# The value weights of the scan: one place, asked for in two halves

## The chip, the cores and the metric

The kernel runs on one core of a Trainium2 chip. The metric is the device time of one execution in microseconds (us). Smaller is better.

## The reference, cut to what matters

The model is an encoder trunk with two layers. Each is a SwiGLU feed-forward, a token mixer and a second feed-forward, with layer norms between. The first layer's mixer is neighbourhood attention. The second's is a bidirectional RWKV-7 time mixing, and the change is in that one.

```python
def rwkv7_bidir(x, mix, w_rkv, ...):          # x: 1 x 512 tokens x 1024 channels
    ...
    xr, xw, xk, xv, xa, xg = (x + xx * mix[i] for i in range(6))
    r = xr @ w_rkv[0]
    k = xk @ w_rkv[1]
    v = xv @ w_rkv[2]                          # the value product
    ...
    def step(state, inp):                      # per direction, 16 heads of 64 channels
        r_t, w_t, k_t, v_t, a_t, b_t = inp
        sa = jnp.einsum('zbhij,zbhj->zbhi', state, a_t)
        state = state * w_t[..., None, :] + sa[..., None] * b_t[..., None, :] + v_t[..., None] * k_t[..., None, :]
        return state, jnp.einsum('zbhij,zbhj->zbhi', state, r_t)
    _, ys = lax.scan(step, jnp.zeros((2, B, H, N, N), f32), xs)
    ...
    return ((y + bonus) * g).astype(x.dtype) @ w_out
```

All numbers are float32.

## The kernel before

The trunk runs as one program of 2200 us: feed-forward, attention, two feed-forwards, the projections of the time mixing, the scan, its output product, and a last feed-forward. The scan takes the stretch from about 1418 to 1803 us.

**Pairs and slots.** The scan works on pairs of heads. A pair (`hp`, 0 to 7) is 128 channels, so it fills the 128 partitions. Tokens come in 8 chunks of 64. The method `slot(n)` runs once per pair, with n from -2 to 7, and in each slot several pairs are at different stages. In slot n the chunk chain runs for pair n (`chain`, thread `c`), the output of pair n - 1 is finished (`finish`, `gate`), the small triangular matrices of pair n + 1 are inverted to the end (`inverted`, `merge`), and for pair n + 2 the decays and factors are made (`front`), the grams, the start of the inversion (`invert`, on GpSimd) and the values (`values`, thread `v`). Pair n + 3 is loaded.

**The order.** Each thread is a generator that yields between its steps. A string per slot (`SEQ`) names the threads in the order in which their next step is written. For TensorE (PE), VectorE (DVE) and ScalarE (ACT) the program keeps that order by hand. GpSimd's (POOL) and SyncE's (SP) instructions are ordered by a planner, from its own estimate of times. SP issues all DMAs, one after the other, so an ask that waits holds back the asks behind it.

**The value product.** For one pair, `values` makes 128 channels x 512 tokens in a PSUM bank: 8 steps, one for each 128 input channels, each of four matmul rows in the trace (`wide`, L1255: two halves of the output channels). Its moving operand is the token tile `xv` (in the trace: `xraw`), its stationary operand the weight tile `wv`, 128 partitions x 8 x 128 numbers, 512 KB. The steps are spread over the slot, between those of the chain. The first `v` in a slot's string writes nothing. The next eight are the steps.

**The weight tile.** There is room for one (`bufs=1`). Behind the last step of a product `weigh` takes the place anew for the next pair and asks for all 512 KB (L1625). A tile that is taken anew waits for every reader of the former one, so the ask waits for the eighth step. The first pair's weights are asked for ahead of the scan's slots, in `receptances`. When the products are done, `outs` takes the place once more, for a part of the output weights (`w_out`).

**Other names that stand in the trace.** L1506 loads the decays `lw` for `front`. L1515 loads the receptance, L1485 and L1488 other inputs of a pair. L1591 and L1592 copy parts of the factors `ar` into the tiles `az` and `xs` that the chain reads. L1703 copies the inverted matrices to `az` in eight small DMAs; they are read by L1758 in the next slot. L1747 to L1766 are the chain: for each chunk, three matmul groups on PE (L1747, L1758, L1764) with ACT (L1751, L1759) between, and DVE's L1766, which makes the next state. L1686 and L1688 are the inversion on POOL, L1679 and L1698 the DVE transposes ahead of it and behind it. L1798 loads output chunks into the token tile `xv` in the slot of the last pair's values.

Of the kernel before, what the change touches and what calls it, by code (L numbers as in the profile page):

```python
# [18 lines left out]
P = 128  # L19
# [4 lines left out]
ND = D // P  # L24
# [78 lines left out]
def flat(ap):  # L103
    return ap.rearrange("p a b -> p (a b)")
# [1015 lines left out]
class Heads:  # L1120
# [114 lines left out]
    def values(self, hp, oT):  # L1235

        k, nc = self.k, self.nc
        po = k.bank()
        for b in range(NB):
            for c in range(2):  # L1240
                for hh in range(2):
                    hs = slice((2 * hp + hh) * HD, (2 * hp + hh + 1) * HD)
                    nc.tensor.matmul(po[HALF[hh], b * P : (b + 1) * P], self.v[b][c][:, hs],
                                     self.pt[hh, b // 2][:, b % 2, c * P : (c + 1) * P], start=c == 0, stop=c == 1)
            if b == NB - 1:
                k.split(*oT.get(hp), halves_of(po))
            yield


class Scan:  # L1250
# [78 lines left out]
    def receptances(self):  # L1329

        nc = self.nc
        one = lambda ap: ap.rearrange("p a b c d -> p (a b c d)")
        az = self.az[2].rearrange("p a b c -> p (a b c)")
        xr = [h[:, i * S : (i + 1) * S] for h, n in ((az, 4), (one(self.units[-2][0]), 2), (one(self.units[-1][0]), 2)) for i in range(n)]
        w = {}

        def load(hp, ap):
            w[hp] = ap.rearrange("p (c f) -> p c f", c=ND)
            self.asked = nc.sync.dma_start(ap, self.w_r[hp]).ins

        def chunk(c):
            nc.sync.dma_start(xr[c], self.dram["xr"][:, c, :])

        for n in ("mask", "onesb"):
            nc.sync.dma_start(getattr(self, n), self.consts[n])
        chunk(0)
        for hp, i in zip(WR_FIRST, (4, 5, 6, 7)):
            load(hp, one(self.units[i][0]))
            if hp == WR_FIRST[0]:
                for c in range(1, ND):  # L1350
                    chunk(c)
                yield
                with self.k.behind(self.asked):
                    self.weigh(0)
            elif hp == WR_FIRST[1]:
                yield
        for _ in range(2):
            self.unit()
        rest = [hp for hp in range(1, ND) if hp not in WR_FIRST]
        order = WR_FIRST + tuple(rest)  # L1360
        while rest:
            pair, rest = rest[:2], rest[2:]
            vt = self.tile("vt", [P, NC, 2, 2, CH], 2)
            for i, hp in enumerate(pair):
                load(hp, one(vt)[:, i * D : (i + 1) * D])
        for i, hp in enumerate(order):
            pr = self.k.bank("ym"[i % 2])
            for c in range(ND):
                self.wide(pr, w[hp][:, c, :], xr[c], c == 0, c == ND - 1)
                if c % 2 and c < ND - 1:  # L1370
                    yield
            t = self.tile(("yh", "yt")[hp % 2], [P, S])
            nc.scalar.activation(t, pr, AF.Copy)
            nc.sync.dma_start(self.dram["rkv"][0][:, hp, :], t)
            if hp == order[-1]:
                self.clear(2)
            yield
# [228 lines left out]
    def values(self, hp):  # L1606

        k, nc, tile_ = self.k, self.nc, self.tile
        p = self.st[hp]
        wv = self.wv  # L1610
        yield
        p.v = tile_("v", [P, S], 2)
        pv = k.bank("a")
        for c in range(ND):
            self.wide(pv, wv[:, c, :], self.xv[:, c, :], c == 0, c == ND - 1)
            if c < ND - 1:
                yield
        nc.scalar.activation(p.v, pv, AF.Copy)
        self.weigh(hp + 1)
        yield  # L1620

    def weigh(self, hp):
        if self.has(hp):
            self.wv = self.tile("wv", [P, ND, P])
            self.nc.sync.dma_start(flat(self.wv), self.w_v[hp])  # L1625

    def gates(self):

# [159 lines left out]
    def outs(self):  # L1788

        nc = self.nc  # L1790
        rows = lambda ap, k: ap[k * P : (k + 1) * P, :]
        w = [self.tile(n, [P, NC, 2, CH]).rearrange("p a b c -> p (a b c)") for n in ("bk1", "ar1")]
        w += [self.az[2][:, i].rearrange("p a b -> p (a b)") for i in range(2)]
        w += [self.tile("wv", [P, ND, P]).rearrange("p a b -> p (a b)")]
        w += [self.units[i][0].rearrange("p a b c d -> p (a b c d)") for i in (2, 4, 3)]
        self.w, self.left = w, [rows(self.dram["x"], t) for t in range(NT)]
        for i in range(EARLY - 1):
            nc.sync.dma_start(self.xv[:, i, :], self.dram["o"][:, i, :])  # L1798
            ask = nc.sync.dma_start(w[i], rows(self.w_out, i)).ins
        yield  # L1800
        for n, (t, h) in enumerate((t, h) for t in range(NT) for h in range(2)):
            hs = slice(h * 512, (h + 1) * 512)
            x = self.tile(("e", "e2", "th")[n % 3], [P, S], 2)
            nc.sync.dma_start(x, rows(self.dram["x"], t)[:, hs])
            acc = self.k.bank("ag"[n % 2])
            for i in range(EARLY):
                if n == 0 and i == EARLY - 1:
                    with self.k.behind(ask):
                        nc.sync.dma_start(self.xv[:, i, :], self.dram["o"][:, i, :])
                        nc.sync.dma_start(w[i], rows(self.w_out, i))  # L1810
                self.wide(acc, self.xv[:, i, t * P : (t + 1) * P], w[i][:, hs], i == 0, i == EARLY - 1)
                if i < EARLY - 1:
                    yield
            nc.vector.scalar_tensor_tensor(x, x, ALPHA, acc, ALU.mult, ALU.add)
            ask = nc.sync.dma_start(rows(self.dram["x"], t)[:, hs], x).ins
            if n == 0:
                with self.k.behind(ask):
                    for c in range(EARLY, ND - 1):
                        nc.sync.dma_start(w[c], rows(self.w_out, c))
            self.stored += 1  # L1820
            self.reload()
            yield
# [214 lines left out]
```

## Time and profile before

| | |
|---|---|
| three runs | 2205.87, 2207.17, 2219.66 us |
| median | 2207.17 us |
| profiled execution, its time | 2204.32 us |
| profiled execution, span from first to last instruction | 2201.7 us |
| mean granted TensorE clock | 0.991 |
| busy share of the span: PE, DVE, ACT, POOL | 97%, 70%, 49%, 24% |

The page's busy share is an average over all stages. A wait names the instruction that waited, and what ended last before it went on. A row of the timeline gives start and length in us, then engine, line, operation, tiles, shapes and count, and in brackets the idle time before it with the one that ended it. The granted clock is the share of full TensorE speed, which falls to 0.5 in some places.

### The profile page before, as it was taken

How to read it: one execution, taken by the hardware profiler on the slowest of the kernel's cores; microseconds unless marked ns; L12 is line 12 of the kernel's file. 1: busy time of each engine (PE TensorE's matmuls, PEld its weight loads, DVE VectorE, ACT ScalarE, POOL GpSimd, SP SyncE). 2: the span in 40 equal slices, each digit the busy share in tenths (PEclk: the TensorE clock that was granted, in tenths of full speed). 3: DMA queues.
4: the chain of work that ended last, by engine and by line, in shares of the span. 5: the costliest groups of instructions: out<-in, count | busy, mean ns of one | idle time of the engine just before them, and what ended most of it. 6: DMA issues, size and time to landing. Idle time of an engine off the chain costs nothing.

```text
span 2201.7 us, 38797 instructions
## 1 busy us (share of the span) xinstructions
PE 2131.1 (97%) x15248; PEld 1726.2 (78%) x15248; DVE 1551.5 (70%) x2506; ACT 1082.2 (49%) x1987; POOL 527.5 (24%) x670
## 2 busy tenths in 40 slices
PE   9999999999999999999999999999998999999998
PEld 8888888887888888787888877446666567788876
DVE  7777767377487777697777779636887558777775
ACT  4444445377344444453444444437776434444443
POOL 1000035555300000520000242046877610000023
PEclk9999999999999999999999999999999999999999
DMA  6544593432334556734555853853544551455583
GB/s 191 174 163 155 177 361 114 117 101 77 113 125 158 159 171 199 298 128 145 159 169 164 311 207 118 293 160 106 135 118 118 169 188 64 152 159 171 163 296 135
DMA packets 160805, 367.81 MB, mean 167 GB/s; under 512 B 32144, under 2 KB 52240, under 8 KB 158576
## 3 DMA queue, kind: packets, MB, share of 16 engines
q1 hardware_dynamic: 160624, 365.36, 50.9%
q8 instruction: 119, 1.95, 0.4%
q14 instruction: 62, 0.51, 0.1%
HBM read 284.29 MB, written 68.94 MB: 160 GB/s over the span
## 4 chain that ended last, share of the span: by engine, by line
PE 63%; DVE 18%; DMA 12%; ACT 3%; issue 2%; POOL 0%; SPq 0%; DVEq 0%; ACTq 0%; POOLq 0%
PE bank L980 13%; PE bank L1063 12%; DMA ra<-in_ffn_w_out_dram 7%; PE a L1255 5%; PE bank L288 5%; PE bank L287 5%; PE bank L289 5%; DVE w L278 4%; PE bank L350 4%; DVE ring L278 2%; ACT w L277 2%; DMA raw<-in_ffn_w_in_dram 2%; PE g L1579 1%; PE y L1255 1%; DVE wx L278 1%
## 5 line engine op out<-in xcount | busy, mean ns | idle before, releaser
L278 POOL TENSOR_TENSOR w<-raw,w 128x1024 fp32r<-128x1024 f32 x38 | 93.4, 2462 | 1206.5 <-ACT w L277 1200.2
L287 PE MATMUL bank<-xT,w 128*128 128x512 f32 x760 | 298.1, 392 | 6.5 <-DVE ar L497 6.5
L278 DVE TENSOR_TENSOR w<-raw,w 128x1024 fp32r<-128x1024 f32 x164 | 200.5, 1223 | 136.4 <-ACT w L277 134.6
L288 PE MATMUL bank<-xT,w 128*128 128x512 f32 x760 | 296.1, 390 | 0.0
L289 PE MATMUL bank<-xT,w 128*128 128x512 f32 x760 | 295.7, 389 | 0.0
L277 ACT ACTIVATE w<-raw 128x1024 fp32r<-128x1024 f32 x202 | 213.0, 1058 | 129.8 <-DMA raw<-in_ffn_w_in_dram 33.6
L1063 PE MATMUL bank<-wx,an 128*128 128x512 f32 x792 | 201.8, 392 | 0.0
L1063 PE MATMUL bank<-w,ring 128*128 128x512 f32 x720 | 171.8, 395 | 7.3 <-DVE w L278 7.3
L287 PEld LDWEIGHTS bank<-xT,w 128*128 128x128 f32 x760 | 142.7, 188 | 37.4 <-DVE ar L497 8.8
L277 ACT ACTIVATE ring<-raw 128x512 fp32r<-128x512 f32 (+1 forms) x99 | 89.3, 904 | 161.5 <-DVE raw L957 119.0
L1063 PEld LDWEIGHTS bank<-w,ring 128*128 128x128 f32 x720 | 136.7, 190 | 38.2 <-DVE w L278 9.0
L289 PEld LDWEIGHTS bank<-xT,w 128*128 128x128 f32 x760 | 142.7, 188 | 30.0
L288 PEld LDWEIGHTS bank<-xT,w 128*128 128x128 f32 x760 | 142.8, 188 | 28.4
L1063 PEld LDWEIGHTS bank<-wx,an 128*128 128x128 f32 x792 | 142.0, 189 | 24.7
L980 PEld LDWEIGHTS bank<-ring,w 128*128 128x128 f32 x864 | 110.8, 191 | 33.4 <-ACT bank L972 30.4
L980 PE MATMUL bank<-ring,w 128*128 128x256 f32 x864 | 119.0, 287 | 15.7 <-ACT bank L972 15.4
L1686 POOL TENSOR_TENSOR tm<-qs,zs 128x126 f32<-128x126 f32 (+22 forms) x248 | 102.8, 414 | 86.9 <-issue 38.9
L1688 POOL TENSOR_TENSOR zs<-zs,tm 128x126 f32<-128x126 f32 (+22 forms) x248 | 112.6, 454 | 19.4
L980 PE MATMUL bank<-ring 128*128 128x256 f32 x864 | 116.3, 284 | 0.1
L980 PEld LDWEIGHTS bank<-ring 128*128 128x128 f32 x864 | 109.6, 193 | 0.4 <-ACT tmp L972 0.4
L495 ACT ACTIVATE tmp<-bank 128x512 f32<-128x512 f32 x52 | 31.1, 597 | 151.8 <-PE bank L289 151.8
L980 PE MATMUL bank<-xT,w 128*128 128x256 f32 x756 | 100.6, 283 | 0.0
(383 smaller groups left out, 4679.4 us busy)
## 6 DMA issues: line engine op xcount, KB each, us to landing
raw<-in_ffn_w_in_dram SPq DMA_DIRECT2D x176, 512.0 KB, 3.7
ra<-in_ffn_w_out_dram SPq DMA_DIRECT2D x44, 1024.0 KB, 5.2
d_away<-away SPq DMA_DIRECT2D x44, 512.0 KB, 4.4
ring<-d_away SPq DMA_DIRECT2D x16, 1024.0 KB, 11.5
xT<-d_late SPq DMA_DIRECT2D x29, 512.0 KB, 8.3
xT<-in_ffn_w_out_dram SPq DMA_DIRECT2D x23, 512.0 KB, 10.0
d_late<-ts SPq DMA_DIRECT2D x44, 256.0 KB, 2.0
d_late<-ra SPq DMA_DIRECT2D x44, 256.0 KB, 2.0
```

Source lines behind the costliest of these rows:

```text
L277: self.hi = self.nc.scalar.activation(h, raw, AF.Copy).ins
L278: self.lo = (eng or self.nc.vector).tensor_tensor(l, raw, h.bitcast(F32), ALU.subtract).ins
L287: nc.tensor.matmul(out, wh, xh, start=start, stop=False)
L288: nc.tensor.matmul(out, wh, xl, start=False, stop=False)
L289: nc.tensor.matmul(out, wl, xh, start=False, stop=stop)
L350: nc.tensor.matmul(acc[t, h], a, u[:, i, h * 512 : (h + 1) * 512], start=first and n == 0, stop=last and n == 2)
L495: nc.scalar.activation(s, pg, AF.Silu)
L980: m = nc.tensor.matmul(out, w[:, i, cs], x[:, j, c], start=start and c + n == 0, stop=c == 3 and n == 2, skip_group_check=True)
L1063: self.nc.tensor.matmul(acc, lhs, u[:, i], start=bool(first) and m == 0, stop=last and m == 2, skip_group_check=more)
L1255: self.nc.tensor.matmul(out[hs], w[:, hs], x, start=start, stop=stop)
L1686: nc.gpsimd.tensor_tensor(tv, qs[:, s, 0:s].rearrange("p (a o) -> p a o", o=1).broadcast_to([P, s, n]), zs[:, s : s + 1, c0:].broadcast_to ...
L1688: nc.gpsimd.tensor_tensor(zs[:, 0:s, c0:], zs[:, 0:s, c0:], tv, ALU.add)
```

## The change

The weight tile is taken once, ahead of the scan, and kept in `self.wv`. The load of a pair's weights becomes two DMAs of 256 KB: input channels of steps 1 to 4, and of steps 5 to 8. The first is written behind the fourth step of the former pair's product, the second where the whole load was, behind the eighth. `outs` uses the kept tile instead of taking the place anew.

```diff
                 with self.k.behind(self.asked):
-                    self.weigh(0)
+                    self.wv = self.tile("wv", [P, ND, P])
+                    for half in range(2):
+                        self.weigh(0, half)
...
         for c in range(ND):
             self.wide(pv, wv[:, c, :], self.xv[:, c, :], c == 0, c == ND - 1)
+            if c == ND // 2 - 1:
+                self.weigh(hp + 1, 0)
             if c < ND - 1:
                 yield
         nc.scalar.activation(p.v, pv, AF.Copy)
-        self.weigh(hp + 1)
-        yield
-
-    def weigh(self, hp):
+        self.weigh(hp + 1, 1)
+        yield
+
+    def weigh(self, hp, half):
         if self.has(hp):
-            self.wv = self.tile("wv", [P, ND, P])
-            self.nc.sync.dma_start(flat(self.wv), self.w_v[hp])
+            cs = slice(half * ND // 2, (half + 1) * ND // 2)
+            self.nc.sync.dma_start(flat(self.wv[:, cs]), self.w_v[hp][:, cs.start * P : cs.stop * P])
...
-        w += [self.tile("wv", [P, ND, P]).rearrange("p a b -> p (a b)")]
+        w += [flat(self.wv)]
```

## The prediction

> **What bounds the kernel now.** I read the page first, then the waits of TensorE in the scan (1418 to 1803 us), then TensorE's rows around each wait. The first fence has the page's span and engines, then a windows row that covers one slot of the scan, the stretch in which pair 4 gets its values.
>
> ```profile
> span 2201.7 us, 38797 instructions
> PE 2131.1 (97%) x15248; PEld 1726.2 (78%) x15248; DVE 1551.5 (70%) x2506; ACT 1082.2 (49%) x1987; POOL 527.5 (24%) x670
> ```
>
> ```profile
> 1576.00:1612.00 36.00, 34.70 (x632) 25.20 (x631) 31.35 (x64) 28.52 (x78) 28.36 (x63) 1.00 0.48 129
> ```
>
> The columns after the length are busy time of PE, its weight loads, DVE, ACT and POOL, then the granted clock, the DMA share and GB/s. In these 36.00 us PE is busy 34.70. So 1.30 us is idle, and next to nothing else is. The other engines have 4.6 us or more left, and the DMA engines half their time. The slot is bound by PE's own list plus that one hole. Who makes the hole is in the waits of PE over the whole scan (us in total, times, longest):
>
> ```profile
> PE a L1255 <- DMA wv<-in_w_rv_dram: 8.9, 4, 3.4
> PE a L1255 <- DVE yt L1837: 2.4, 1, 2.4
> ```
>
> and in PE's timeline, where the first step of the value product of pairs 2 to 7 looks like this:
>
> ```profile
> 1510.86 1.03 PE L1255 MATMUL a<-xraw,wv 128*64 128x512 f32 x4
> ...
> 1546.89 1.08 PE L1255 MATMUL a<-xraw,wv 128*64 128x512 f32 x4 [1.87 <-DMA wv<-in_w_rv_dram]
> ...
> 1582.88 1.08 PE L1255 MATMUL a<-xraw,wv 128*64 128x512 f32 x4 [1.30 <-DMA wv<-in_w_rv_dram]
> ...
> 1619.93 1.23 PE L1255 MATMUL a<-xraw,wv 128*64 128x512 f32 x4 [2.40 <-DVE yt L1837]
> ...
> 1659.54 1.97 PE L1255 MATMUL a<-xraw,wv 128*64 128x512 f32 x4 [3.35 <-DMA wv<-in_w_rv_dram]
> ...
> 1699.25 1.98 PE L1255 MATMUL a<-xraw,wv 128*64 128x512 f32 x4 [2.40 <-DMA wv<-in_w_rv_dram]
> ```
>
> Pair 2 has no wait. Pairs 3, 4, 6 and 7 wait 1.87, 1.30, 3.35 and 2.40 us for the weights. Pair 5's 2.40 is put down to a DVE instruction that its matmul doesn't read. I give it to the weights too, because of the ask on SP and its time to landing:
>
> ```profile
> 1613.51 0.92 SPq L1625 DMA_DIRECT2D wv<-in_w_rv_dram  x1
> ```
>
> ```profile
> DMA to landing us min/median/max: 6.3/6.3/6.3
> ```
>
> 1613.51 + 6.3 is 1619.8, and the product starts at 1619.93. So the weights end **five waits, 11.32 us** together.
>
> The 1.97 in pair 6, where pair 4 has 1.08 for the same four matmuls, is a second loss. The windows behind the waits of pairs 4 to 7 show it in the granted clock (the third number from the right):
>
> ```profile
> 1582.50:1586.50 4.00, 3.62 (x54) 2.42 (x56) 2.58 (x5) 1.42 (x4) 3.49 (x7) 1.00 0.68 196
> ...
> 1619.90:1624.60 4.70, 4.67 (x44) 2.92 (x46) 1.08 (x2) 1.29 (x4) 4.03 (x9) 0.64 0.50 136
> ...
> 1659.50:1665.30 5.80, 5.76 (x44) 3.17 (x46) 0.13 (x1) 1.45 (x4) 4.86 (x12) 0.52 0.33 102
> ...
> 1699.20:1702.80 3.60, 3.55 (x32) 2.09 (x32) 1.25 (x3) 0.28 (x1) 3.13 (x7) 0.53 0.89 288
> ```
>
> After 1.30 us of idleness the clock stays 1.00; after 2.40, 3.35 and 2.40 it is 0.64, 0.52 and 0.53 on average. What that costs is the distance from the first step to the chain's next state product (L1764), a fixed list of instructions:
>
> ```profile
> 1586.10 0.40 PE L1764 MATMUL m<-vt,tb 128*64 128x64 f32 x8
> ...
> 1624.67 0.40 PE L1764 MATMUL m<-vt,tb 128*64 128x64 f32 x8
> ...
> 1665.33 0.40 PE L1764 MATMUL m<-vt,tb 128*64 128x64 f32 x8
> ...
> 1703.81 0.40 PE L1764 MATMUL m<-vt,tb 128*64 128x64 f32 x8
> ```
>
> Pair 4 needs 1586.10 - 1582.88 = 3.22 us at full clock, pair 5 4.74, pair 6 5.79, pair 7 4.56. The excess is 1.52, 2.57 and 1.34 (pair 7's slot has a shorter list, so its 1.34 is a floor): **5.43 us**.
>
> **The change, part by part.** *The first half.* It is asked for behind step 4 of the former product, not behind step 8. For the slot of pair 3, whose product is followed by pair 4's, steps 4, 5 and 8 stand here in PE's timeline, with the old ask on SP:
>
> ```profile
> 1556.27 1.08 PE L1255 MATMUL a<-xraw,wv 128*64 128x512 f32 x4
> ...
> 1565.33 1.08 PE L1255 MATMUL a<-xraw,wv 128*64 128x512 f32 x4
> ...
> 1574.31 1.03 PE L1255 MATMUL a<-xraw,wv 128*64 128x512 f32 x4
> ```
>
> ```profile
> 1570.36 5.28 SPq L1703 DMA_DIRECT2D az<-qd  x8
> ...
> 1577.90 0.38 SPq L1625 DMA_DIRECT2D wv<-in_w_rv_dram  x1
> ```
>
> Step 8 ends at 1575.3, yet the whole load is asked at 1577.90, because SP is busy with the eight asks of L1703 and two more. It lands too late for 1581.58, when PE is free for it. The first half can be asked from 1557.4, some 24 us before that moment. Even twice the 6.3 us of the slowest landing leaves over 11 us. So the first step's wait goes.
>
> *The second half.* It is asked where the whole one is now, and it is needed at step 5, which comes 1565.33 - 1546.89 = 18.4 us after step 1. With the old ask at 1577.90 and 6.3 us it would be there at 1584, and step 5 of pair 4 runs near 1600. It costs nothing, and it is half of what then competes with the other loads. That cover is gone only if SP gives the ask some 15 us later than now.
>
> *The kept tile.* A reader of one half must not be made to wait for the load of the other, and the first half's ask must need step 4 alone. The trace has the same pattern on the token tile in pair 7: the output chunks are loaded into slices of it that the product has read, while the product still reads later slices.
>
> ```profile
> 1705.67 0.54 SPq L1798 DMA_DIRECT2D xraw<-d_o  x1
> ```
>
> ```profile
> 1707.18 1.08 PE L1255 MATMUL a<-xraw,wv 128*64 128x512 f32 x4
> ```
>
> ```profile
> DMA to landing us min/median/max: 2.8/2.9/2.9
> ```
>
> The load asked at 1705.67 lands at about 1708.5; the product's step at 1707.18 reads the same tile and didn't wait. So slices are followed one by one, and this costs nothing. If they weren't, step 5 would wait for the first half; it follows step 4 by 8 us here, and a landing takes 6.3, so only the slot in which the two steps adjoin would pay, some 6 us once.
>
> *One more ask on SP, eight times (seven in the slots, one at the start).* 0.4 to 0.9 us each by the rows above. In the slots they stand between asks that PE isn't waiting for, so I take 0. The bound is 8 x 0.9 = 7 us, if each pushed back a load that PE then waited for.
>
> *What is late next.* DVE must keep up, since the next state (L1766) follows each L1764. These are its rows in the slots of pairs 4 and 6:
>
> ```profile
> 1586.55 0.61 DVE L1766 TENSOR_TENSOR vt<-m,pc 64x128 f32<-64x128 f32 x2 [1.40 <-PE m L1764]
> ```
>
> ```profile
> 1665.77 0.61 DVE L1766 TENSOR_TENSOR vt<-m,pc 64x128 f32<-64x128 f32 x2 [6.14 <-PE m L1764]
> ```
>
> DVE waited 1.40 where PE will come 1.30 earlier, and 6.14 where it will come 3.35 + 2.57 = 5.92 earlier. So 0.1 to 0.2 us of slack is left: it fits, barely. I charge 0.1 us in each of five slots, 0.5 in all (bounds 0 and 5: DVE's 31.35 us in a slot of 34.7 can't itself be a bound).
>
> **The sum.** 11.32 + 5.43 - 0.5 = 16.2 us. The profiled execution took 2204.32 us (span 2201.7), so **2188.1**. The runs' median is 2207.17, 2.85 above it. That may be more clock loss at the same waits, which the changed kernel wouldn't have, so I don't add it and forecast **2188**, 0.87% under the median.
>
> A rule of the Trainium skill bears on the clock term. "TensorE: Matmul & The Clock Gate", Part 1, says that the clock falls to half after an idle window of about 3.4 us, and that the window is free-running. The two waits of 2.40 that were followed by 0.64 and 0.53 disagree with the length; that losses differ after equal waits agrees with free running. By the length alone only pair 6 would have lost, and the sum would be 11.32 + 2.57 = 13.9 us, an estimate of 2190.
>
> **The rivals.** *1. The hole is only partly closed.* POOL has the smallest room behind DVE. It inverts one pair per slot, and one round starts and ends here, with DVE's reader of its result behind:
>
> ```profile
> 1569.53 0.24 POOL L1686 TENSOR_TENSOR tm<-qs,zs 128x31 f32<-128x31 f32 x1 [2.86 <-issue]
> ```
>
> ```profile
> 1602.56 0.22 POOL L1688 TENSOR_TENSOR zs<-zs,tm 128x16 f32<-128x16 f32 x1
> ```
>
> ```profile
> 1605.43 1.02 DVE L1698 STREAM_TRANSPOSE qd<-zs 128x512 f32<-128x512 f32 x1
> ```
>
> A round takes 33.25 us, and its reader comes 2.65 us later. A slot that shrinks by 1.30 to 34.7 us leaves about 1.3. For: both margins are thin, and POOL and DVE could slow each other when packed closer. Against: both remain positive. If each of five slots keeps 1 to 2 us, the gain is 6 to 11: 2193 to 2198. Chance 0.13.
>
> *2. Given back later.* The scan ends 16 us sooner, but the loads behind it don't. For: the DMA share is 0.48 in a slot. Against: that is half, and those loads wait for buffers that the same slots free, so they move along. It would give 2204 to 2207. Chance 0.07.
>
> *3. Slower: the second half gets ahead of L1703.* The planner orders SP by its own times. Step 8 ends at 1575.3 and L1703's asks run from 1570.36; were the second half placed ahead of them, SP would stand until 1575.3, and the eight asks would end at 1581. Their landing and the reader in the next slot:
>
> ```profile
> az<-qd SPq DMA_DIRECT2D x64, 32.0 KB, 2.0
> ```
>
> ```profile
> 1579.61 0.27 PE L1758 MATMUL c<-wr,az 64*64 64x64 f32 x1
> ```
>
> 1581 + 2.0 is 3.4 us past 1579.61; with pair 6's clock loss, 2.57, that is 6.0 per slot, 36 in six slots, against 16 gained: 2224. It decides from 2 us of delay on. Against: the ask stands behind L1703 now, and nothing moves it forward. Chance 0.03.
>
> *4. More than the sum*, if fewer idle stretches also spare the clock elsewhere: 2179 to 2183. Chance 0.05.
>
> **How the numbers follow.** The forecast has 0.72, with 2184 to 2192 as its own range. The range that should hold 8 in 10 takes in most of rival 1 and the bound of the extra asks: **2183 to 2199**. A measurement of this kernel can tell about 1%, 22 us, from no change. Under 2185.1 lie rival 4 and the lowest tenth of the forecast: 0.13. Above 2229 there is only a worse rival 3: 0.03. Within 1%: 0.84.
>
> **What would show it.** Right: no wait of PE for these weights from pair 3 on, the first steps 34.7 us apart, clock 1.00 in the windows behind them, two asks per pair on SP, the second behind L1703. Wrong: a wait of the first step that names DVE or a bank, a wait at step 5, L1758 waiting for L1703's loads, POOL's rounds without an idle gap, or the same first steps 36 us and more apart.

## The result and the profile after

The changed kernel took 2190.27 us in the median, against 2205.87 for the kernel before beside it, a ratio of **0.9918** with an interval of 0.989 to 0.9947. The forecast was 2188, 2.3 us less. Two further comparisons gave 0.9931 (0.9908 to 0.9954) and 0.9941 (0.9924 to 0.9958). Line numbers behind `weigh` are 4 higher in the profile after (L1764 is L1768, L1703 is L1707, and so on).

The page after, and the windows row of the slot that answers to the one shown of before:

```profile
span 2185.1 us, 38811 instructions
...
PE 2121.4 (97%) x15248; PEld 1720.4 (79%) x15248; DVE 1552.4 (71%) x2506; ACT 1081.4 (49%) x1987; POOL 529.9 (24%) x670
```

```profile
1575.00:1610.00 35.00, 34.95 (x634) 25.07 (x632) 31.89 (x63) 28.61 (x79) 28.74 (x63) 1.00 0.51 135
```

PE is now busy in 34.95 of 35.00 us: the hole is gone, and the clock is 1.00. The span is 16.6 us shorter, and PE's busy time fell by 9.7 us although its instructions are the same in number. In the slots (1510.86 to 1725.50 before, 1508.34 to 1706.20 after) PE was busy for 203.3 us at a mean clock of 0.97 before, and for 197.6 at 1.00 after. So 5.7 us of the 9.7 are matmuls there that no longer run at a lower clock; the rest lies outside the slots. The first value steps of pairs 2 to 7:

```profile
1508.34 1.05 PE L1255 MATMUL a<-xraw,wv 128*64 128x512 f32 x4
...
1542.41 1.03 PE L1255 MATMUL a<-xraw,wv 128*64 128x512 f32 x4
...
1576.79 1.03 PE L1255 MATMUL a<-xraw,wv 128*64 128x512 f32 x4
...
1611.70 1.03 PE L1255 MATMUL a<-xraw,wv 128*64 128x512 f32 x4
...
1646.65 1.03 PE L1255 MATMUL a<-xraw,wv 128*64 128x512 f32 x4
...
1681.06 1.03 PE L1255 MATMUL a<-xraw,wv 128*64 128x512 f32 x4
```

None has a wait behind it, and from pair 2 on they are 34.1, 34.4, 34.9, 35.0 and 34.4 us apart. On SP, the ask of the first half stands behind step 4 (1555.36), that of the second where the whole load stood, behind the eight asks of the inverted matrices:

```profile
1555.36 0.46 SPq L1629 DMA_DIRECT2D wv<-in_w_rv_dram  x1
...
1565.82 5.26 SPq L1707 DMA_DIRECT2D az<-qd  x8
...
1573.73 0.38 SPq L1629 DMA_DIRECT2D wv<-in_w_rv_dram  x1
```

From 1500 to 1700 us the halves land 2.5 to 4.8 us behind their ask:

```profile
DMA to landing us min/median/max: 2.5/3.9/4.8
```

**Where the 16.6 us lie.** From the first step of pair 2 to the last of pair 7 the kernel before took 214.1 us (1510.86 to 1725.00), the changed one 197.4 (1508.34 to 1705.72): 16.8 us gained, where the sum said 16.2. Ahead of that the changed kernel was 2.5 us early. Behind it, 2.7 us are missing: 2.0 of them up to the first row of the last output product (L1446 before, L1448 after), 0.6 later. That the whole span comes so near to the sum is therefore in part luck: these two, which the sum doesn't have, nearly cancel. The experiments show what of this belongs to the change.

### The profile page after: what moved, and what is told of

It reads as the page before. It is cut to its first block, busy times and chain, and to the rows that moved or that the text cites. A ratio compares the mean times of both kernels' runs of the same rounds, so it can differ in the third digit from the quotient of the medians.

```text
span 2185.1 us, 38811 instructions
## 1 busy us (share of the span) xinstructions
PE 2121.4 (97%) x15248; PEld 1720.4 (79%) x15248; DVE 1552.4 (71%) x2506; ACT 1081.4 (49%) x1987; POOL 529.9 (24%) x670
## 5 line engine op out<-in xcount | busy, mean ns | idle before, releaser
L277 ACT ACTIVATE w<-raw 128x1024 fp32r<-128x1024 f32 x202 | 213.1, 1058 | 129.2 <-DMA raw<-in_ffn_w_in_dram 34.9
L1690 POOL TENSOR_TENSOR tm<-qs,zs 128x126 f32<-128x126 f32 (+22 forms) x248 | 108.8, 439 | 65.0 <-DVE qs L1683 26.8
```

Source lines behind the costliest of these rows:

```text
L277: self.hi = self.nc.scalar.activation(h, raw, AF.Copy).ins
L1690: nc.gpsimd.tensor_tensor(tv, qs[:, s, 0:s].rearrange("p (a o) -> p a o", o=1).broadcast_to([P, s, n]), zs[:, s : s + 1, c0:].broadcast_to ...
```

## The experiments

**Both kernels again, for a second profile.** The kernel before:

> The kernel before once more, for a second profile. Theory: the five waits for the value weights are there again, 1 to 3.5 us each and 10 to 13 us together, since the order on SP causes them; which of them are followed by a low clock may differ, by 0 to 2.6 us each. Rival: the waits themselves come and go by more than a microsecond from one execution to the next.

The ratio was 1.000 (0.9983 to 1.0016). The five waits were 2.18, 2.08, 3.42, 3.89 and 2.55 us, 14.1 together where the first profile had 11.3. So the waits were there again, but their sizes moved by up to 1.02 us for one pair (pair 5). The total is above the 10 to 13 us that I had expected, one wait is above 3.5, and the rival isn't excluded for single pairs. Two of them, with the windows behind them:

```profile
1581.17 1.71 PE L1255 MATMUL a<-xraw,wv 128*64 128x512 f32 x4 [2.08 <-DMA wv<-in_w_rv_dram]
...
1585.96 0.40 PE L1764 MATMUL m<-vt,tb 128*64 128x64 f32 x8
```

```profile
1620.78 1.08 PE L1255 MATMUL a<-xraw,wv 128*64 128x512 f32 x4 [3.42 <-DMA wv<-in_w_rv_dram]
1624.00 0.40 PE L1764 MATMUL m<-vt,tb 128*64 128x64 f32 x8
```

```profile
1581.10:1586.00 4.90, 4.83 (x46) 3.08 (x48) 1.56 (x3) 1.06 (x4) 4.27 (x9) 0.65 0.47 142
1620.70:1624.00 3.30, 3.22 (x45) 2.05 (x47) 0.11 (x1) 1.02 (x4) 2.75 (x8) 1.00 0.37 114
```

Behind 2.08 us of idleness the clock fell to 0.65 and the same list took 4.79 us; behind 3.42 us it stayed 1.00 and the list took 3.22. The slots took 218.9 us here, against 214.1 in the first profile. The changed kernel:

> The changed kernel once more, for a second profile. Theory: pairs 2 to 7 have no wait of the first value step, first steps are 34.4 to 35.0 us apart, and the ratio to before is 0.989 to 0.995. The 2.5 us that the first profile had gained ahead of the first value step (a shorter wait for the receptance weights and no clock fall behind it) are a matter of the execution: here they may be there or not. Rival: they belong to the change and are there again.

> The changed kernel, beside the other three on the same chip: ratio to before 0.990 to 0.994, no wait of the first value step from pair 3 on, 81 us from the last value step to L1448.

No wait from pair 3 on in either. The slots took 197.5 and 196.8 us, so the changed kernel's three profiles agree within 0.7 us where the kernel before differs by 4.8. The first step of pair 0 began at 1423.22 and 1424.28, and at 1424.31 in the second profile of the kernel before: the 2.5 us that were gained ahead of the slots belong to the execution (in the first profile of before, a wait of 2.13 us for the receptance weights was followed by a low clock). From the last value step to the last output product it is 79.1 and 80.0 us before, and 81.1, 81.0 and 79.6 after (I had expected 81): up to 2 us given back, or nothing.

**Kept tile alone.** What was asked first is whether the early ask does it, or one of the other two things that the change brings: the kept place and the smaller loads.

```diff
+                    self.wv = self.tile("wv", [P, ND, P])      # once, ahead of the scan
...
-            self.wv = self.tile("wv", [P, ND, P])
             self.nc.sync.dma_start(flat(self.wv), self.w_v[hp])
```

> The tile is kept in one place, but all 512 KB are asked for behind the eighth step, as before. Theory (the early ask of the first half brings the gain): the waits of the first step for pairs 3 to 7 stay, 1 to 3.5 us each, 9 to 12 us together, and the time is that of the kernel before, ratio 0.998 to 1.002. Rival (taking the tile anew for each pair was what held the ask back): the waits fall below 4 us together and the ratio is near 0.993.

Ratio 0.9987 (0.9971 to 1.0003), waits of 10.4 us in pairs 3 to 7. The kept place alone is worth nothing that can be measured.

**Both halves written behind step 8, tile kept.**

```diff
-            if c == ND // 2 - 1:
-                self.weigh(hp + 1, 0)
...
+        self.weigh(hp + 1, 0)
         self.weigh(hp + 1, 1)
```

> The tile is kept and the load is split, but both halves are asked for behind the eighth step. Theory (the gain comes from asking early, and splitting gives what a smaller load saves in landing): 256 KB loads land in about 4 us where 512 KB land in 5 to 6, so each of the five waits shrinks by 1 to 2 us, 3 to 6 us of wait are left, the clock falls at one place at most, and the ratio is about 0.995. Rival 1 (the split alone is enough): no waits, ratio 0.992. Rival 2 (DMA engines are full at that moment, both halves share them and land together): waits as before, ratio 1.000.

Ratio 0.9926 (0.9904 to 0.9949), no wait. That is the outcome that the first rival named, but SP's timeline gives another reason. First this kernel's, then the changed one's:

```profile
1552.36 0.40 SPq L1508 DMA_DIRECT2D lw<-d_lw  x1
1552.86 0.46 SPq L1628 DMA_DIRECT2D wv<-in_w_rv_dram  x1
1553.41 1.11 SPq L1490 DMA_DIRECT2D gt<-d_iv  x2
```

```profile
1554.86 0.41 SPq L1508 DMA_DIRECT2D lw<-d_lw  x1
...
1555.90 1.11 SPq L1490 DMA_DIRECT2D gt<-d_iv  x2
```

The ask stands in the same place, between L1508 and L1490, some 18 us ahead of the second half's. The planner moves an ask to where its operands are free. Since the kept tile is followed slice by slice, the first half is free behind step 4, wherever the line is written. So this kernel didn't ask late, and it tests none of the three readings. Two more kernels do hold the ask back.

**Split, but taken anew.** The tile is taken for each pair as before, so both halves wait for step 8.

```diff
             self.wv = self.tile("wv", [P, ND, P])
-            self.nc.sync.dma_start(flat(self.wv), self.w_v[hp])
+            for half in range(2):
+                cs = slice(half * ND // 2, (half + 1) * ND // 2)
+                self.nc.sync.dma_start(flat(self.wv[:, cs]), self.w_v[hp][:, cs.start * P : cs.stop * P])
```

> The kernel before with the load split: the tile is taken anew for each pair, so both 256 KB asks wait for the eighth step and stand next to each other on SP, the half of steps 1 to 4 first. Theory (what brings the gain is that the first half is asked for some 16 us earlier): the first step still waits in pairs 3 to 7, though less, since half the bytes land sooner: 3 to 8 us together instead of 11 to 14, ratio 0.994 to 0.998. Rival (the smaller first load is enough): no waits, ratio 0.992 to 0.993.

Ratio 0.9952 (0.9932 to 0.9971). Its asks, next to each other (x2), and PE's waits in the scan:

```profile
1573.85 0.86 SPq L1627 DMA_DIRECT2D wv<-in_w_rv_dram  x2
```

```profile
PE a L1255 <- DMA wv<-in_w_rv_dram: 4.8, 4, 2.3
```

4.8 us of wait are left, within the 3 to 8 that the theory named. So half the bytes in front bring over half of the gain without any early ask. Beside it on the same chip the changed kernel has 0.9941, and the two intervals overlap. By medians it is 10.3 us gained here (2192.03) and 16.5 there (2185.82), and every run here (from 2188.49) is longer than every one there (up to 2187.91). That difference is what the early ask adds, with the kept tile that it needs.

**Kept, the half of steps 1 to 4 held behind the other.**

```diff
         self.weigh(hp + 1, 1)
+        with k.behind(*[self.weighed] if self.has(hp + 1) else ()):
+            self.weigh(hp + 1, 0)
```

`self.weighed` is the load that was written last, and `behind` keeps the next one behind it.

> The changed kernel with its two asks next to each other behind the eighth step, the half of steps 5 to 8 first and that of steps 1 to 4 behind it. The tile is kept. Theory (the early ask): the first half now lands as late as the whole load did, the waits of pairs 3 to 7 are back with 10 to 15 us together, ratio 0.997 to 1.002. Rival (kept tile and smaller loads bring the gain): ratio 0.992 to 0.994.

Ratio 1.0001 (0.9979 to 1.0023), with the waits back:

```profile
PE a L1255 <- DMA wv<-in_w_rv_dram: 8.9, 4, 3.0
...
PE a L1255 <- DVE vt L1770: 0.8, 1, 0.8
```

That is 9.7 us with the one put down to DVE, a little under the 10 to 15 expected. Kept tile, split and one more ask per pair are all in it, and the gain is gone. What counts is how early the half that is read first lands.

**The clock by itself.** The kernel before, with idle matmuls ahead of step 1 of pairs 3 to 7, in a bank that the step overwrites:

```diff
         pv = k.bank("a")
+        if hp >= 3:
+            k.busy(pv, 8)
```

> The kernel before with eight idle matmuls (128x128, about 1.1 us together) ahead of the first value step of pairs 3 to 7, into the bank that the step then overwrites. The loads are as before. Theory (the slow matmuls behind the waits are a second loss, of the clock, caused by idleness): the weights arrive when they did, so the 11.3 us without value work stay, but idle time is 1.1 us shorter each; the clock stays at or near 1.00 for pairs 5 and 7 and falls at most for pair 6; 3 to 5.4 us are gained, ratio 0.9975 to 0.9985. Rival (the matmuls are slow because the DMA traffic of that moment slows them): the same low clock or the same long matmuls, and the ratio is 1.000 or above.

Ratio 0.997 (0.9949 to 0.999), 6.6 us. That is more than the 3 to 5.4 us that I had expected, though the interval takes them in. Pair 5's slot and its window:

```profile
1612.70 2.05 PE L387 MATMUL a<-ident 128*128 128x128 f32 x16
...
1615.91 1.08 PE L1255 MATMUL a<-xraw,wv 128*64 128x512 f32 x4 [1.16 <-DMA wv<-in_w_rv_dram]
```

```profile
1615.90:1620.00 4.10, 4.09 (x56) 2.43 (x57) 0.85 (x4) 1.87 (x5) 3.47 (x9) 1.00 0.37 115
```

The idle matmuls take 2.05 us, not the 1.1 that I had reckoned. In pairs 4 to 7 the weights still come 0.4 to 1.3 us behind them, in pair 3 just as they end. The clock is 1.00 in the windows behind all five, with DMA shares of 0.37 to 0.70. In the first profile of before, the shares behind the waits of pairs 4 and 6 were 0.68 and 0.33, and the clock 1.00 and 0.52. So the slow matmuls are the clock's, not the traffic's.

**What bounds it next: attempts at the output product.** In the changed kernel the longest waits of the scan are those for the output weights:

```profile
PE a L1255 <- DMA bk<-in_rw_out_dram: 3.4, 1, 3.4
PE a L1255 <- DMA ar<-in_rw_out_dram: 2.5, 1, 2.5
```

The first attempt moved the first output steps behind four chain steps, and read `ar` fourth:

```diff
-    6: "x c o o o c c o n c o x o c o n c c ...
+    6: "x c c c n c x c o o o o o o o n c c ...
```

> The changed kernel with the first output products moved: six of their steps in slot 6 are written behind four more chain steps, and the chunk whose weights come last (ar) is read fourth, not second. Theory (the 2.1 us given back behind the last value product are PE standing at the output weights): the two waits of 3.4 and 2.5 us and the half clock behind them shrink to under 3 us together, and 2 to 5 us are gained over the changed kernel, ratio to before about 0.990. Rival (the chain is late there itself, so that PE has nothing else to do): waits of the same sum with other names, ratio as the changed kernel's, 0.992.

Ratio 0.9946 (0.9929 to 0.9963), no gain. From the last value step to the last output product it took 83.0 us: the waits came back under other names, the chain's among them. The second attempt left the order of steps, read `ar` fourth and put idle matmuls into the wait:

```diff
-        w += [self.az[2][:, i].rearrange("p a b -> p (a b)") for i in range(2)]
+        w[1:1] = [self.az[2][:, i].rearrange("p a b -> p (a b)") for i in range(2)]
...
             acc = self.k.bank("ag"[n % 2])
+            if n == 0:
+                self.k.busy(acc, 12)
```

> The changed kernel with twelve idle matmuls (about 1.5 to 3 us) ahead of the first output product, in the wait for its weights, and the chunk whose weights come last (ar) read fourth. Theory (behind the last value step PE stands some 6 us, and the clock falls to half behind it): the clock stays up for the first output steps, and from the last value step to the last product's first row (L1448) it is 79 us or less instead of 81; ratio to before 0.990 to 0.992. Rival (these steps wait for loads in any case, and a full clock only makes the next wait longer): 81 us again.

> The version with the idle matmuls ahead of the first output product once more, with more rounds. Theory (its gain over the changed kernel lies in the last feed-forward, where one wait of 3.8 us was 0.9 and the clock stayed up, and it comes with this program): the wait is 0.9 again, ratio to before 0.989 to 0.992. Rival (it was a matter of that execution): 3.8 again, ratio 0.992 to 0.994.

> The changed kernel with the one chunk order of the output product alone (ar read fourth), without idle matmuls. Theory (the idle matmuls are what matters near the output product, and they gain nothing there): 81 us from the last value step to L1448, as with them. In the last feed-forward either 3.8 (then the idle matmuls moved it) or 0.9 (then the order did).

With the idle matmuls the ratio was 0.9913 (0.9886 to 0.9939), and with more rounds **0.9898** (0.9877 to 0.992), the lowest of all. The first interval overlaps that of the changed kernel beside it (0.9924 to 0.9958), though each of its four runs (up to 2180.41 us) is shorter than each of that kernel's seven (from 2183.13). The reason that I gave is wrong: up to the last output product it took 81.2 and 83.2 us, no better. From there to the end of the span it is 392.9 and 393.8 us, against 398.2 to 398.3 in the changed kernel's three profiles. That gain is in the last feed-forward, where one wait of PE is 0.9 us (0.7 in the second profile) instead of 3.8. First this version's row, then the changed kernel's:

```profile
PE bank L1063 <- DVE w L278: 0.9, 1, 0.9
```

```profile
PE bank L1063 <- DVE w L278: 3.8, 1, 3.8
```

With the chunk order alone the ratio is 0.992 (0.9891 to 0.9949) and the wait 3.8 again, as in every other profile here, so it is the idle matmuls that move it, 400 us further on. In the changed kernel two of DVE's operations ahead of that wait take 2.58 and 2.97 us, here 1.45 and 1.21, and POOL's next to them lie otherwise. Why this program sets them so stays open. (With the chunk order alone the output product started from a profile that was 12 us late ahead of the scan, and its 82.1 us there say no more than "not 79".)

## Why the prediction was right

**The waits.** Right: 11.32 us were to go and went; no first step waits in any of three profiles of the changed kernel. The giving of pair 5's wait to the weights holds, since it went with the others.

**The clock.** Right that it is a second loss, and right in size for that execution: 5.43 us in the sum, 5.7 less of PE's busy time in the slots. Pair 7's list took 3.05 us in the changed kernel (1681.06 to 1684.11), so its excess was 1.51, above the floor of 1.34. The losses of another execution differ: in the second profile of before they were some 7 us, behind the waits of pairs 3, 4, 6 and 7. What I left out of the forecast, that other runs of the kernel before may lose more, is what that profile shows. By the same reckoning waits and clock of that profile would have summed to some 21 us. By medians the changed kernel gained 15.6, 18.2 and 16.5 us in its three comparisons, so that the sum came so near is also luck in the profile that it was read from.

**Second half, kept tile, extra asks.** Right. There is no wait at step 5, slices are followed one by one, and eight more asks cost nothing that shows.

**What is late next.** The right place, and a size that was too small. The rows of DVE that follow the first step and the next ones in the slot of pair 4, and those of PE that read what they write:

```profile
1580.64 0.61 DVE L1770 TENSOR_TENSOR vt<-m,pc 64x128 f32<-64x128 f32 x2
...
1584.29 0.61 DVE L1770 TENSOR_TENSOR vt<-m,pc 64x128 f32<-64x128 f32 x2
```

```profile
1581.06 0.64 PE L1751 MATMUL c<-vt,xs 128*64 128x64 f32 x7
...
1584.63 0.71 PE L1751 MATMUL c<-vt,xs 128*64 128x64 f32 x7
```

The first of them answers to DVE's row at 1586.55 in the prediction. The 1.40 us of waiting is gone and no slack is left: DVE comes straight from other work, 0.69 us behind the start of the state product (1579.95), where it was 0.45 before. PE shows no idle time there, but its rows are longer, 0.64 and 0.71 us against 0.40 and 0.51 in the kernel before (1587.20 and 1590.47). Step 4 comes 9.96 us after step 1 in pair 4 and 10.00 in pair 5, against 9.36 and 9.35 in pairs 3 and 6, and 9.50 in pair 4 of the kernel before. That is 0.5 to 0.6 us in each of two slots, about 1.1 in all, where the sum charged 0.1 in each of five. In the other two profiles of the changed kernel the distance is 10.0 us in pairs 4 and 6, and in pair 4 alone. The rows point to DVE; no run tested it by itself. The slots gained some 0.5 us more than the sum in spite of it, and where that came from stays open. POOL's round and DVE's reader of its result:

```profile
1598.00 0.55 POOL L1692 TENSOR_TENSOR zs<-zs,tm 128x16 f32<-128x16 f32 x1
1599.96 0.24 POOL L1690 TENSOR_TENSOR tm<-qs,zs 128x31 f32<-128x31 f32 x1 [1.41 <-issue]
```

```profile
1599.75 1.01 DVE L1702 STREAM_TRANSPOSE qd<-zs 128x512 f32<-128x512 f32 x1
```

POOL ends its round 1.2 us ahead of its reader (1.3 was forecast).

**The rivals.** "Partly closed" and "the second half ahead of L1703" didn't come: the asks stand as assumed. The price of the latter was not tried. "Given back later" came at most in small, 0 to 2 us, at the output weights.

**One thing that I took for granted and that is not so.** I treated "written behind step 4" as the cause. The kernel with both halves written behind step 8 is as fast: the planner places the ask by what it depends on. What the early ask needs is a tile that isn't taken anew, and a load that touches only the slices already read. Nor did I price the smaller first load by itself, which gave 10.3 of 16.5 us where both were measured on one chip.

## What to carry to other kernels

A load that waits for the last reader of its only buffer can be asked for earlier without a second buffer: keep the tile, split the load along the order in which it is read, and ask for each part when its slices are free. The split alone may give a good part of it. Look at where the asks stand in the queue, not at where they are written: a planner may have moved them already, and an experiment that moves the line may then test nothing. And count a short PE wait twice when pricing it: by its length, and by what the clock does to the matmuls behind it.

## What the runs showed of the hardware

Idle stretches of PE of 2.08 and 2.40 us were followed by half clock for some 3 us, while one of 3.42 us was not, nor those of 1.30 and 1.87 in the first profile of before. The length of a gap alone doesn't decide; the cost of one gap was 0 or 1.5 to 2.6 us. "TensorE: Matmul & The Clock Gate" of the Trainium skill, Part 1, says that the activity window is free-running; that gaps of like length cost differently agrees with it, though no run here shows the window itself. Its rule there, that idle gaps shouldn't exceed about 3.4 us, isn't enough in this kernel: gaps of 2.08 and 2.40 us lost the clock.

Idle matmuls of 2.05 us inside waits of 2.1 to 3.3 us kept the clock at 1.00 in all five places, which makes them a cheap remedy where the wait itself can't be removed.
